# Feature-major chunks of a two-block kernel: from 256-column matmuls into one bank to 512-column and 256-column matmuls into two

## The chip, the cores and the metric

The kernel runs on one core of a Trainium2 chip. The metric is the device time of one execution in microseconds (us). One execution was profiled as well, and every row below is of that execution.

The engines are called as in the profile: PE is TensorE (matmuls), PEld its weight loads, DVE is VectorE, ACT is ScalarE, POOL is GpSimd, and SP issues the weight DMAs. Matmul results land in PSUM, which ACT and DVE read out.

## The reference

A sequence of 256 tokens with 1024 features goes through a first block and then twice through a hybrid layer. What matters here are projections of the normalised tokens:

```python
# first block
h = rms_norm(x, g_mix)
c_h, c_b, c_c, sq, sk, sv, xq, gate_pre = split(h @ w_in)
y_conv = (c_b * causal_depthwise_conv(c_c * c_h, conv_w)) @ w_conv_out
o_sb = stick_breaking_attention(heads(sq), heads(sk), heads(sv))   # 16 heads of 64
...
# hybrid layer, twice
fq, fk, fv, f_logit, rq, rk, rv, rg = split(x @ w_in)
fox_out = fox_attention(fq, fk, fv, log_sigmoid(f_logit + b_forget))  # 8 heads of 64
ret_out = silu(rg) * head_groupnorm(retention(rotary(rq), rotary(rk), rv))
x = layernorm(alpha * x + concat(fox_out, ret_out) @ w_out)
x = layernorm(alpha * x + square(relu(x @ w_ff1)) @ w_ff2)
```

## The kernel before

**Split operands.** Every float32 operand of a large matmul is held as two parts, hi (rounded by a cast to fp32r) and lo (the rest). A product is three matmuls: hi x hi, hi x lo and lo x hi. The activations of a stage lie in one tile `xT` of 128 partitions x 8 k-tiles x 2 parts x 256 tokens; `x[0]` is its hi part, `x[1]` its lo part, and `x[2]` both parts side by side, 512 elements for each k-tile.

**Weights.** `Stream` brings the weights in the order of use, in chunks of 1 MB and as two halves ("pieces"). For each piece ACT casts the raw data to `whi` (L218) and DVE subtracts to get `wlo` (L224). `tick()` is called between pieces of PE's work. It advances the side generators by one step (attention heads and the like) and then splits one or two more weight pieces. No scheduler moves anything: each engine runs its instructions in the order in which the code is written, and semaphores are the only waits.

**Feature-major chunks.** 32 chunks of 256 output features are computed with the features on the partitions by `stream_a` (L386): `sq`, `sk`, `ch`, `cc`, `cb` in each of four groups of the first block (loop `for i in range(4)`), and `fq`, `fk`, `rg`, two of each, in both hybrid layers. A chunk consists of two column tiles of 128 features (`nt` = 0 and 1). `unit_a` writes one column tile in 24 matmuls of 256 columns: for each of 8 k-tiles whi with `x[0]`, whi with `x[1]`, wlo with `x[0]`. Both column tiles go into the two halves of one PSUM bank, and the caller reads the bank directly (ACT casts, DVE subtracts or multiplies).

**PSUM.** `acc()` hands out four banks in turn. The pool takes the bank that has been free longest in program order, and PE waits until the bank's last reader is done. The chunks, the transposes `to_T` and the value products of the heads (`o = acc()` in `sb_pair` and `fox_pair`) all draw on these four. Scores and the heads' transposes use the other four banks (`aux`).

**One stick-breaking pair** (`sb_pair`, two heads). A step of PE writes the scores of both heads (12 matmuls, L348). ACT then computes abs, exp and ln (L611 to L613), DVE the sum `e`, a scan and a difference (`e`, `r`, `r`), ACT an exp (L619), DVE the causal mask (`r<-r,dmask`). Some ticks later PE transposes `r` (L628), ACT copies it to `pt`, and PE multiplies with the values (`acc<-pt,v`). In each group, the first pair's scores lie in the middle of `cc`, and its transposes in the middle of the next group's `sq`. There the second pair's scores follow right behind. The first pair's value product comes between the next `sk` and the next `ch`. The tick at the middle of a chunk calls the side steps ahead of the chunk's own eviction, so that what a pair computes on DVE stands in DVE's queue ahead of the chunk's readers.

**Wide chunks elsewhere.** The MLPs' up-projections use `stream_w` (L368): 16 matmuls of 512 columns, both banks first, and then 16 of 256.

Of the kernel before, what the change touches and what calls it, by code (L numbers as in the profile page):

```python
# [9 lines left out]
F32 = mybir.dt.float32  # L10
F32R = mybir.dt.float32r
BF16 = mybir.dt.bfloat16
AF = mybir.ActivationFunctionType
ALU = mybir.AluOpType
# [3 lines left out]
S = 256  # L18
# [235 lines left out]
def block_kernel(ctx: ExitStack, tc: tile.TileContext, a: dict, out: bass.AP, upto=None, dbg=None):  # L254
    nc = tc.nc
    ctx.enter_context(tc.manual_schedule())

    def pool(stack, name, bufs=1, side="left", space=None):
        kw = {} if space is None else {"space": space}
        return stack.enter_context(tc.tile_pool(name=name, bufs=bufs, side=side, reuse_waits="tile", **kw))  # L260
# [16 lines left out]
    def acc():  # L277
        return accp.tile([128, 512], F32, tag="acc", name="acc")
# [9 lines left out]
    def bank():  # L288
        assert cur_ps[0][1] == 1
        return cur_ps[0][0].tile([128, 512], F32, tag="bank", name="bank")  # L290
# [3 lines left out]
    W = Stream(nc, rp, wp, a["wpack"])  # L294
    sides = []

    def tick(n=1):
        for g in list(sides):
            if next(g, "end") == "end":
                sides.remove(g)  # L300
        W.pump(n)
# [17 lines left out]
    def act_set(name):  # L319
        if cur_set[0] != name:  # L320
            nc.scalar.preload_act_table_set(name)
            cur_set[0] = name

    def tt(o, x, y, op):
        nc.vector.tensor_tensor(o, x, y, op=op)  # L325

    def stt(o, x, s, y, op0, op1):
        nc.vector.scalar_tensor_tensor(out=o, in0=x, scalar=s, in1=y, op0=op0, op1=op1)  # L328

    def split(hi, lo, src):  # L330
        nc.scalar.copy(hi, src)  # L331
        tt(lo, src, hi.bitcast(F32), ALU.subtract)

    def split_scaled(hi, lo, src, s):
        nc.scalar.mul(hi, src, s)
        stt(lo, src, s, hi.bitcast(F32), ALU.mult, ALU.subtract)

    def mm3(o, lh, ll, rh, rl, first, last):
        nc.tensor.matmul(o, lhsT=lh, rhs=rh, start=first, stop=False, skip_group_check=True)  # L339
        nc.tensor.matmul(o, lhsT=lh, rhs=rl, start=False, stop=False, skip_group_check=True)  # L340
        nc.tensor.matmul(o, lhsT=ll, rhs=rh, start=False, stop=last, skip_group_check=True)  # L341
# [9 lines left out]
    def mm(o, l, r, first=True, last=True):  # L351
        nc.tensor.matmul(o, lhsT=l, rhs=r, start=first, stop=last, skip_group_check=True)  # L352

    def unit_a(o, w, nt, x):
        for k in range(8):
            ns = slice(nt * 128, nt * 128 + 128)
            mm3(o, w[0][:, k, ns], w[1][:, k, ns], x[0][:, k, :], x[1][:, k, :], k == 0, k == 7)
# [25 lines left out]
                W.free()  # L383
            evict(nt, ps[nt].rearrange("p (s t) -> p t s", s=2))

    def stream_a(key, x):  # L386
        w = W.get(key)
        p = acc()
        pv = p.rearrange("p (n t) -> p n t", n=2)
        unit_a(pv[:, 0, :], w, 0, x)  # L390
        tick()
        unit_a(pv[:, 1, :], w, 1, x)
        W.free()
        return pv

    def stream_b(key, x, evict=None):

        p = [acc(), acc()]
        for j in range(2):
            w = W.get((*key, j))  # L400
            for t in range(2):
                unit_b(p[t], w, t, x, 4 * j, j == 0, j == 1)
                if t:
                    W.free()
                if j and evict is not None:
                    evict(t, p[t])
                if not (j and t):
                    tick()
        return p
# [57 lines left out]
    def new_xT():  # L467

        xT = ap.tile([128, 8, 2, S], F32R, tag="xT", name="xT")
        return xT[:, :, 0, :], xT[:, :, 1, :], xT  # L470


    hT = new_xT()
# [13 lines left out]
    def turned(t, h, p):  # L487
        transposes(p, ht[t][:, hs[h]], 4)
        return p.rearrange("p (k t) -> p k t", k=4)
# [25 lines left out]
    p = turned(0, 0, acc())  # L515
# [7 lines left out]
    w = W.peek()  # L523
    term(p0, w, 0, 0, 0, 0, True)
    p = turned(0, 1, acc())
# [13 lines left out]
    w = W.peek()  # L539
# [6 lines left out]
    p = turned(1, 0, acc())  # L546
# [11 lines left out]
    p = turned(1, 1, acc())  # L558
# [26 lines left out]
    sp = pool(st1, "sb", side="right")  # L585
# [55 lines left out]
        split(osb[0][:, pair, :], osb[1][:, pair, :], o[:, 0:256])  # L641

    for i in range(4):
        p = stream_a(("sq", i), hT)
        split_scaled(qs[0], qs[1], p, 0.125)
        tick()
        p = stream_a(("sk", i), hT)
        split(kb[0], kb[1], p)
        tick()
        sides.append(sb_pair(i, 0, 2, 3))  # L650
        sides.append(sb_pair(i, 1, 6, 4))
        p = stream_a(("ch", i), hT)
        chs = sp.tile([128, 2, S], F32, tag="chs", name="chs")
        nc.scalar.copy(chs, p)
        tick()
        p = stream_a(("cc", i), hT)
        tt(u[:, :, 2:], p, chs, ALU.mult)
        cv = sp.tile([128, 2, S], F32, tag="cv", name="cv")
        for nt in range(2):
            ct = 2 * i + nt  # L660
            nc.vector.tensor_scalar(cv[:, nt, :], u[:, nt, 0:S], cw[:, ct, 0:1], None, op0=ALU.mult)
            stt(cv[:, nt, :], u[:, nt, 1:S + 1], cw[:, ct, 1:2], cv[:, nt, :], ALU.mult, ALU.add)
            stt(cv[:, nt, :], u[:, nt, 2:S + 2], cw[:, ct, 2:3], cv[:, nt, :], ALU.mult, ALU.add)
        tick()
        p = stream_a(("cb", i), hT)
        tt(cv, p, cv, ALU.mult)
        split(yc[0][:, 2 * i:2 * i + 2, :], yc[1][:, 2 * i:2 * i + 2, :], cv)
        tick()
# [45 lines left out]
    for n in range(2):  # L714
        ns = slice(512 * n, 512 * n + 512)
# [3 lines left out]
        def evict(t, p):  # L719
            tt(sg[:, t, :], p, sg[:, t, :], ALU.mult)  # L720
            tt(merged[:, t, ns], merged[:, t, ns], sg[:, t, :], ALU.add)
# [90 lines left out]
    for h in range(2):  # L812
        box = {}
        p = stream_b(("xk", h), memT)
# [3 lines left out]
        p = stream_b(("xq", h), hT)  # L818
        box["qn"] = qk_prep(p, gq, "q")
        tick()  # L820
        p = stream_b(("xv", h), memT)
# [255 lines left out]
    xT = x2T[0]  # L1077
    for l in range(2):
        st = ExitStack()
        p2 = pool(st, f"mix{l}")  # L1080

        def T(shape, dt, tag, bufs=1):
            return p2.tile(shape, dt, tag=tag, name=tag, bufs=bufs)
# [23 lines left out]
        for t in range(2):  # L1107
            pk = bank()
            for i in range(2):
                p = bank()  # L1110
# [68 lines left out]
        fp = pool(fst, f"fox{l}", side="right")  # L1179
# [54 lines left out]
            split(mix[0][:, pair, :], mix[1][:, pair, :], o[:, 0:256])  # L1234

        for i in range(2):
            p = stream_a((l, "fq", i), xT)
            split_scaled(fqs[0], fqs[1], p, 0.125)
            tick()
            p = stream_a((l, "fk", i), xT)  # L1240
            split(fkb[0], fkb[1], p)
            tick()
            for nt in range(2):
                fox.append(fox_pair(i, nt, *((0, 1, 4, 9), (0, 4, 7, 10), (1, 3, 6, 8), (4, 6, 8, 10))[2 * i + nt]))
            sides.extend(fox[-2:])
# [70 lines left out]
        rgt = T([128, 4, S], F32, "rkT")  # L1316
        ret = ret_side()
        sides.append(ret)
        for i in range(2):
            p = stream_a((l, "rg", i), xT)  # L1320
            s = rgt[:, 2 * i:2 * i + 2, :]
            act_set(SILU)
            nc.scalar.activation(s, p, AF.Silu)
            rgs[f"s{i}"] = s
            tick()
        nT = [None]
# [71 lines left out]
        xT = nT2[0]  # L1398
# [33 lines left out]
```

## Time and profile before

| | before |
|---|---|
| time, median of 3 runs | 1201.65 us (1201.48 to 1204.26) |
| the profiled execution | 1200.3 us, of which the span of the instructions is 1198.5 us |
| PE busy | 1189.2 us (99% of the span) |
| PEld busy | 1028.2 us (86%) |
| DVE busy | 790.7 us (66%) |
| ACT busy | 630.6 us (53%) |
| HBM | 181 GB/s over the span |
| granted PE clock | 0.999 of full speed |

"Busy" is a union of the instructions' intervals. A PE interval includes the way through the array and overlaps the next one, so the distance between starts tells PE's pace. A group's mean duration does not.

### The profile page before, as it was taken

What the parts mean: (1) busy time and instruction counts of PE and PEld (TensorE: products, weight loads), DVE (VectorE), ACT (ScalarE), POOL (GpSimd) and SP (SyncE); (2) the same over time, 40 slices, a digit from 0 to 9 for tenths busy, and PEclk for the clock granted to TensorE, in tenths of its full rate; (3) what the DMA queues carried; (4) which work ended last, traced back from release to release, by engine and by line L of the source; (5) the groups of instructions that cost most, each with busy time, mean ns of one, the idle gap of its engine ahead of it and who ended that gap; (6) DMA issues with size and microseconds to landing.
All of it is one profiled execution on the core that took longest, in us unless ns stands there. A gap on an engine that the chain in (4) does not pass through costs nothing.

```text
span 1198.5 us, 17236 instructions
## 1 busy us (share of the span) xinstructions
PE 1189.2 (99%) x6832; PEld 1028.2 (86%) x6832; DVE 790.7 (66%) x1036; ACT 630.6 (53%) x883; POOL 27.6 (2%) x46
## 2 busy tenths in 40 slices
PE   9999999999999999999999999999999999999997
PEld 6999988888888888888898888888889888888886
DVE  6678775656666667566566686656667668675563
ACT  6565556445554556455255555645535555664550
POOL 1000000000000100000000100000000010000000
PEclk9999999999999999999999999999999999999999
DMA  7654447654456566546454465655545436656530
GB/s 297 231 176 140 131 153 235 229 213 142 152 164 221 187 206 225 193 176 234 154 161 139 132 213 201 212 210 176 208 145 186 145 119 217 213 199 223 166 133 35
DMA packets 60354, 218.40 MB, mean 182 GB/s; under 512 B 6849, under 2 KB 7121, under 8 KB 60274
## 3 DMA queue, kind: packets, MB, share of 16 engines
q1 hardware_dynamic: 58176, 210.46, 51.6%
q0 software_dynamic: 1808, 6.45, 1.7%
q8 instruction: 53, 0.87, 0.3%
q10 hardware_dynamic: 290, 0.40, 0.1%
q14 instruction: 27, 0.22, 0.1%
HBM read 216.23 MB, written 1.05 MB: 181 GB/s over the span
## 4 chain that ended last, share of the span: by engine, by line
PE 99%; DVE 0%; POOLq 0%; issue 0%; DVEq 0%
PE acc L352 22%; PE acc L339 12%; PE acc L341 12%; PE acc L340 12%; PE bank L339 11%; PE bank L341 11%; PE bank L340 11%; PE acc L450 2%; PE bank L352 1%; PE aux L348 1%; PE aux L1222 0%; PE acc L435 0%; PE aux L628 0%; PE aux L340 0%; PE aux L341 0%; PE aux L339 0%
## 5 line engine op out<-in xcount | busy, mean ns | idle before, releaser
L224 DVE TENSOR_TENSOR wlo<-raw,whi 128x1024 fp32r<-128x1024 f32 x392 | 464.5, 1220 | 75.6 <-ACT whi L218 73.5
L218 ACT CAST whi<-raw 128x1024 fp32r<-128x1024 f32 x392 | 394.1, 1049 | 75.1 <-PE bank L341 36.9
L352 PE MATMUL acc<-xT,whi 128*128 128x512 f32 x672 | 160.2, 390 | 0.0
L339 PE MATMUL bank<-whi,hid 128*128 128x512 f32 (+1 forms) x388 | 150.6, 388 | 0.5 <-DVE x L328 0.5
L340 PE MATMUL bank<-wlo,hid 128*128 128x512 f32 (+1 forms) x388 | 150.3, 387 | 0.0
L341 PE MATMUL bank<-whi,hid 128*128 128x512 f32 (+1 forms) x388 | 150.1, 387 | 0.0
L339 PE MATMUL acc<-xT,whi 128*128 128x256 f32 x512 | 147.6, 288 | 0.0
L352 PEld LDWEIGHTS acc<-xT,whi 128*128 128x128 f32 x672 | 124.4, 188 | 24.8
L340 PE MATMUL acc<-xT,whi 128*128 128x256 f32 x512 | 144.8, 283 | 0.0
L341 PE MATMUL acc<-xT,wlo 128*128 128x256 f32 x512 | 144.7, 283 | 0.0
L922 ACT ACTIVATE r<-r 128x512 f32<-128x512 f32 x42 | 26.6, 633 | 157.5 <-DVE r L968 157.5
L339 PEld LDWEIGHTS acc<-xT,whi 128*128 128x128 f32 x512 | 98.0, 191 | 1.9 <-issue 1.0
L340 PEld LDWEIGHTS acc<-xT,whi 128*128 128x128 f32 x512 | 98.1, 192 | 0.2
L341 PEld LDWEIGHTS acc<-xT,wlo 128*128 128x128 f32 x512 | 98.0, 191 | 0.0
L352 PEld LDWEIGHTS acc<-xT,wlo 128*128 128x128 f32 x672 | 85.9, 191 | 3.0
L352 PE MATMUL acc<-xT,wlo 128*128 128x256 f32 x672 | 87.4, 283 | 0.0
L339 PEld LDWEIGHTS bank<-whi,hid 128*128 128x128 f32 x388 | 72.9, 188 | 15.0 <-DVE x L328 0.7
L341 PEld LDWEIGHTS bank<-whi,hid 128*128 128x128 f32 x388 | 72.8, 188 | 15.0
L968 DVE TENSOR_REDUCE r<-acc 128x256 f32<-128x512 f32 x84 | 55.5, 686 | 44.7 <-PE acc L352 44.7
L340 PEld LDWEIGHTS bank<-wlo,hid 128*128 128x128 f32 x388 | 72.9, 188 | 14.1
L325 DVE TENSOR_TENSOR hid<-r,hid 128x512 fp32r<-128x512 f32 x42 | 29.1, 692 | 84.8 <-ACT hid L331 84.8
L339 PE MATMUL acc<-whi,xT 128*128 128x512 f32 x208 | 83.4, 401 | 0.0
(293 smaller groups left out, 1734.3 us busy)
## 6 DMA issues: line engine op xcount, KB each, us to landing
raw<-in_wpack_dram SPq DMA_DIRECT2D x388, 512.0 KB, 4.5
raw<-in_wpack_dram SPq DMA_DIRECT2D x4, 528.0 KB, 4.6
gb<-in_ln_g_dram POOLq DMA_DIRECT2D x4, 512.0 KB, 3.8
bb<-in_ln_b_dram POOLq DMA_DIRECT2D x4, 512.0 KB, 5.8
x<-in_x_dram SPq DMA_DIRECT2D x3, 512.0 KB, 5.8
mem<-in_mem_dram SPq DMA_DIRECT2D x2, 512.0 KB, 6.1
cst<-in_c_dram POOLq DMA_DIRECT2D x1, 898.0 KB, 7.6
out_dram<-x SPq DMA_DIRECT2D x3, 256.0 KB, 2.1
```

Of the source, the lines that this page charges most:

```text
L218: nc.scalar.copy(hi, raw)
L224: self.nc.vector.tensor_tensor(lo, raw, hi.bitcast(F32), op=ALU.subtract)
L325: nc.vector.tensor_tensor(o, x, y, op=op)
L339: nc.tensor.matmul(o, lhsT=lh, rhs=rh, start=first, stop=False, skip_group_check=True)
L340: nc.tensor.matmul(o, lhsT=lh, rhs=rl, start=False, stop=False, skip_group_check=True)
L341: nc.tensor.matmul(o, lhsT=ll, rhs=rh, start=False, stop=last, skip_group_check=True)
L348: nc.tensor.matmul(o[:, h, :], lhsT=q[a][hs[h]], rhs=k[b][hs[h]], start=i == 0, stop=i == 2, skip_group_check=True)
L352: nc.tensor.matmul(o, lhsT=l, rhs=r, start=first, stop=last, skip_group_check=True)
L450: nc.tensor.transpose(o[:, k * 128:(k + 1) * 128], src[:, k * 128:(k + 1) * 128], ident)
L922: nc.scalar.activation(dst, src, AF.Relu)
L968: lambda nt, h: nc.vector.tensor_reduce(rv[:, nt, :], h, AX.X, ALU.add))
```

## The change

`stream_s` takes the place of `stream_a`. Each column tile gets a bank of its own, in which the two halves are the two products with the hi and the lo part of x. Eight matmuls of 512 columns (whi with `x[2]`) fill the bank, and eight of 256 columns (wlo with `x[0]`) accumulate onto the first half. After each column tile ACT copies the first half to an SBUF tile, and DVE adds the second half onto it. The middle `tick()` comes after the first column tile's eviction. The callers then read the SBUF tile in place of PSUM, and Silu runs in place on it.

```diff
--- before.py
+++ after.py
@@ -383,15 +383,26 @@
                 W.free()
             evict(nt, ps[nt].rearrange("p (s t) -> p t s", s=2))
 
-    def stream_a(key, x):
+    def stream_s(key, x, dst):
+
+        def evict(nt, h):
+            nc.scalar.copy(dst[:, nt, :], h[:, :, 0])
+            tt(dst[:, nt, :], h[:, :, 1], dst[:, nt, :], ALU.add)
+
         w = W.get(key)
-        p = acc()
-        pv = p.rearrange("p (n t) -> p n t", n=2)
-        unit_a(pv[:, 0, :], w, 0, x)
-        tick()
-        unit_a(pv[:, 1, :], w, 1, x)
-        W.free()
-        return pv
+        for nt in range(2):
+            p = acc()
+            ns = slice(nt * 128, nt * 128 + 128)
+            for k in range(8):
+                mm(p.rearrange("p (s t) -> p s t", s=2), w[0][:, k, ns], x[2][:, k], k == 0, False)
+            for k in range(8):
+                mm(p[:, 0:S], w[1][:, k, ns], x[0][:, k, :], False, k == 7)
+            if nt:
+                W.free()
+            evict(nt, p.rearrange("p (s t) -> p t s", s=2))
+            if not nt:
+                tick()
+        return dst
 
     def stream_b(key, x, evict=None):
 
@@ -641,19 +652,17 @@
         split(osb[0][:, pair, :], osb[1][:, pair, :], o[:, 0:256])
 
     for i in range(4):
-        p = stream_a(("sq", i), hT)
+        p = stream_s(("sq", i), hT, sp.tile([128, 2, S], F32, tag="st", name="st", bufs=2))
         split_scaled(qs[0], qs[1], p, 0.125)
         tick()
-        p = stream_a(("sk", i), hT)
+        p = stream_s(("sk", i), hT, sp.tile([128, 2, S], F32, tag="st", name="st", bufs=2))
         split(kb[0], kb[1], p)
         tick()
         sides.append(sb_pair(i, 0, 2, 3))
         sides.append(sb_pair(i, 1, 6, 4))
-        p = stream_a(("ch", i), hT)
-        chs = sp.tile([128, 2, S], F32, tag="chs", name="chs")
-        nc.scalar.copy(chs, p)
+        chs = stream_s(("ch", i), hT, sp.tile([128, 2, S], F32, tag="chs", name="chs"))
         tick()
-        p = stream_a(("cc", i), hT)
+        p = stream_s(("cc", i), hT, sp.tile([128, 2, S], F32, tag="st", name="st", bufs=2))
         tt(u[:, :, 2:], p, chs, ALU.mult)
         cv = sp.tile([128, 2, S], F32, tag="cv", name="cv")
         for nt in range(2):
@@ -662,7 +671,7 @@
             stt(cv[:, nt, :], u[:, nt, 1:S + 1], cw[:, ct, 1:2], cv[:, nt, :], ALU.mult, ALU.add)
             stt(cv[:, nt, :], u[:, nt, 2:S + 2], cw[:, ct, 2:3], cv[:, nt, :], ALU.mult, ALU.add)
         tick()
-        p = stream_a(("cb", i), hT)
+        p = stream_s(("cb", i), hT, sp.tile([128, 2, S], F32, tag="st", name="st", bufs=2))
         tt(cv, p, cv, ALU.mult)
         split(yc[0][:, 2 * i:2 * i + 2, :], yc[1][:, 2 * i:2 * i + 2, :], cv)
         tick()
@@ -1234,10 +1243,10 @@
             split(mix[0][:, pair, :], mix[1][:, pair, :], o[:, 0:256])
 
         for i in range(2):
-            p = stream_a((l, "fq", i), xT)
+            p = stream_s((l, "fq", i), xT, fp.tile([128, 2, S], F32, tag="st", name="st", bufs=2))
             split_scaled(fqs[0], fqs[1], p, 0.125)
             tick()
-            p = stream_a((l, "fk", i), xT)
+            p = stream_s((l, "fk", i), xT, fp.tile([128, 2, S], F32, tag="st", name="st", bufs=2))
             split(fkb[0], fkb[1], p)
             tick()
             for nt in range(2):
@@ -1317,10 +1326,9 @@
         ret = ret_side()
         sides.append(ret)
         for i in range(2):
-            p = stream_a((l, "rg", i), xT)
-            s = rgt[:, 2 * i:2 * i + 2, :]
+            s = stream_s((l, "rg", i), xT, rgt[:, 2 * i:2 * i + 2, :])
             act_set(SILU)
-            nc.scalar.activation(s, p, AF.Silu)
+            nc.scalar.activation(s, s, AF.Silu)
             rgs[f"s{i}"] = s
             tick()
         nT = [None]
```

**First place: DVE in the middle of the second group's `sq` chunk.** Before, this is DVE's order from the last weight piece ahead of the second pair's work (`e`, `r`) to the next `kb` (numbers are buffers, `acc` a PSUM bank, `aux` the scores):

```order
L224 TENSOR_TENSOR wlo_689<-raw_541,whi_688 128x1024
L328 SCALAR_TENSOR_TENSOR e_772<-aux_759,e_772 128x768
L615 SCALAR_TENSOR_TENSOR r_773<-smask_369,e_772 128x768
L325 TENSOR_TENSOR r_773<-aux_759,r_773 128x768
L224 TENSOR_TENSOR wlo_781<-raw_571,whi_780 128x1024
L328 SCALAR_TENSOR_TENSOR q1_374<-acc_725,q0_373 128x512
L325 TENSOR_TENSOR r_773<-r_773,dmask_370 128x2x256
L224 TENSOR_TENSOR wlo_781<-raw_623,whi_780 128x1024
L224 TENSOR_TENSOR wlo_844<-raw_661,whi_843 128x1024
L325 TENSOR_TENSOR kb1_376<-acc_818,kb0_375 128x512
```

In the changed kernel, from the same weight piece on; `st<-acc,st` is the new addition, `acc_674` and `acc_729` are the banks of the first and the second column tile of `sq`, and `acc_757` is that of the first of `sk`:

```order
L224 TENSOR_TENSOR wlo_642<-raw_516,whi_641 128x1024
L325 TENSOR_TENSOR st_673<-acc_674,st_673 128x256
L328 SCALAR_TENSOR_TENSOR e_715<-aux_702,e_715 128x768
L626 SCALAR_TENSOR_TENSOR r_716<-smask_369,e_715 128x768
L325 TENSOR_TENSOR r_716<-aux_702,r_716 128x768
L224 TENSOR_TENSOR wlo_724<-raw_539,whi_723 128x1024
L325 TENSOR_TENSOR st_673<-acc_729,st_673 128x256
L328 SCALAR_TENSOR_TENSOR q1_374<-st_673,q0_373 128x512
L325 TENSOR_TENSOR r_716<-r_716,dmask_370 128x2x256
L224 TENSOR_TENSOR wlo_724<-raw_586,whi_723 128x1024
L325 TENSOR_TENSOR st_756<-acc_757,st_756 128x256
L224 TENSOR_TENSOR wlo_777<-raw_619,whi_776 128x1024
```

The reader of `sq`'s one bank (`q1<-acc`) stood behind the pair's `e`, `r`, `r` and a weight piece; now the last reader of the second column tile's bank stands there. How many banks PE takes between this chunk and the next `ch` has changed too.

**PE at the same place.** Before, from the last matmul of `sk` (bank `acc_818`) over the values (`acc_875`) to the first of `ch` (`acc_886`), with the semaphores that each waits for:

```order
L341 MATMUL acc_818<-xT_124,wlo_538 128x256
L352 MATMUL acc_875<-pt_757,v_237 64x256 [waits Activation_49]
L352 MATMUL acc_875<-pt_757,v_237 64x128
L352 MATMUL acc_875<-pt_757,v_237 64x256
L352 MATMUL acc_875<-pt_757,v_237 64x128
L339 MATMUL acc_886<-xT_124,whi_619 128x256 [waits DVE_49]
```

In the changed kernel, from the end of the second column tile of `sq` (`acc_729`) to the first matmul of `ch` (`acc_815`):

```order
L352 MATMUL acc_729<-xT_124,wlo_462 128x256 x8
L352 MATMUL acc_757<-xT_124,whi_512 128x512 [waits DVE_49]
L352 MATMUL acc_757<-xT_124,whi_512 128x512 x7
L352 MATMUL acc_757<-xT_124,wlo_513 128x256 x8
L352 MATMUL acc_782<-xT_124,whi_512 128x512 [waits DVE_49]
L352 MATMUL acc_782<-xT_124,whi_512 128x512 x7
L352 MATMUL acc_782<-xT_124,wlo_513 128x256 x8
L352 MATMUL acc_803<-pt_700,v_237 64x256 [waits DVE_49,Activation_49]
L352 MATMUL acc_803<-pt_700,v_237 64x128
L352 MATMUL acc_803<-pt_700,v_237 64x256
L352 MATMUL acc_803<-pt_700,v_237 64x128
L352 MATMUL acc_815<-xT_124,whi_582 128x512 [waits DVE_49]
```

Between `sq` and `ch`, PE took the banks of `sq`, `sk` and the values, and `ch` the fourth. Now `acc_729`, two banks of `sk` and one of the values are four, and `acc_815` of `ch` is the fifth, which takes the bank of `acc_729`.

**Second place: PE at the second `rg` chunk of layer 0.** Before, from the middle of the chunk (bank `acc_6321`) over a value product of the fox heads (`acc_6346`) and the transposes of the normalised retention output for the first 128 tokens (`on_6261`), back to the chunk:

```order
L341 MATMUL acc_6321<-xT_5199,wlo_6012 128x256
L352 MATMUL acc_6346<-fpt_6224,ta_5919 64x256 [waits DVE_49]
L352 MATMUL acc_6346<-fpt_6224,ta_5919 64x128
L352 MATMUL acc_6346<-fpt_6224,ta_5919 64x256
L352 MATMUL acc_6346<-fpt_6224,ta_5919 64x128
L450 MATMUL acc_6353<-ident_62,on_6261 128x128 [waits Activation_49]
L450 MATMUL acc_6353<-ident_62,on_6261 128x128 x3
L339 MATMUL acc_6321<-xT_5199,whi_6011 128x256
```

In the changed kernel, from the last matmuls of the first column tile (`acc_6062`) on:

```order
L352 MATMUL acc_6062<-xT_4991,wlo_5764 128x256 x8
L352 MATMUL acc_6081<-fpt_5970,ta_5671 64x256 [waits DVE_49]
L352 MATMUL acc_6081<-fpt_5970,ta_5671 64x128
L352 MATMUL acc_6081<-fpt_5970,ta_5671 64x256
L352 MATMUL acc_6081<-fpt_5970,ta_5671 64x128
L461 MATMUL acc_6088<-ident_62,on_6007 128x128 [waits DVE_49]
L461 MATMUL acc_6088<-ident_62,on_6007 128x128 x3
L352 MATMUL acc_6100<-xT_4991,whi_5763 128x512 [waits DVE_49]
```

The rest of the chunk continued in a bank that it held already; its second column tile now starts a new bank (`acc_6100`) and waits for DVE. The transposes (`acc_6088`) waited for ACT and now wait for DVE.

## Rows read from the trace of the kernel before

**Rows 1.** The page: busy time by engine, and the chain that ended last

```profile
PE 1189.2 (99%) x6832; PEld 1028.2 (86%) x6832; DVE 790.7 (66%) x1036; ACT 630.6 (53%) x883; POOL 27.6 (2%) x46
...
PE 99%; DVE 0%; POOLq 0%; issue 0%; DVEq 0%
```

**Rows 2.** Timeline, TensorE: start, length, line, instruction, shape, count

```profile
521.44 3.79 PE L352 MATMUL acc<-xT,whi 128*128 128x512 f32 x16
525.06 2.08 PE L352 MATMUL acc<-xT,wlo 128*128 128x256 f32 x16
526.98 3.36 PE L352 MATMUL acc<-xT,whi 128*128 128x512 f32 x14
```

**Rows 3.** Windows, one group: PE, PEld, DVE, ACT, POOL, clock, DMA

```profile
52.80:86.00 33.20, 33.20 (x287) 32.28 (x286) 25.88 (x31) 19.98 (x25) 0.00 (x0) 1.00 0.43 140
```

**Rows 4.** Timeline, ScalarE and VectorE: a cast and a subtraction out of PSUM

```profile
79.75 0.37 ACT L331 CAST osbh<-acc 128x256 fp32r<-128x256 f32 x1
...
81.72 0.41 DVE L325 TENSOR_TENSOR osbl<-acc,osbh 128x256 fp32r<-128x256 f32 x1
```

**Rows 5.** Timeline, TensorE, from the first pair's transposes to the values

```profile
65.28 0.84 PE L628 MATMUL aux<-ident,r 128*128 128x128 f32 x6
66.05 0.91 PE L348 MATMUL aux<-kb,q 64*128 64x256 f32 x12
...
75.71 0.88 PE L352 MATMUL acc<-pt,v 128*64 128x256 f32 x8
```

**Rows 6.** Timeline, VectorE, the same stretch

```profile
64.50 0.68 DVE L325 TENSOR_TENSOR r<-r,dmask 128x512 f32<-128x512 f32 x1
...
67.38 0.68 DVE L325 TENSOR_TENSOR cv<-acc,cv 128x512 f32<-128x512 f32 x1
...
72.86 0.96 DVE L328 SCALAR_TENSOR_TENSOR e<-aux,e 128x768 f32<-128x768 f32 x1 [1.94 <-ACT e L613]
...
75.64 0.96 DVE L325 TENSOR_TENSOR r<-aux,r 128x768 f32<-128x768 f32 x1
76.52 1.22 DVE L224 TENSOR_TENSOR wlo<-raw,whi 128x1024 fp32r<-128x1024 f32 x1
77.65 0.68 DVE L328 SCALAR_TENSOR_TENSOR q<-acc,q 128x512 fp32r<-128x512 f32 x1
78.25 0.68 DVE L325 TENSOR_TENSOR r<-r,dmask 128x512 f32<-128x512 f32 x1
```

**Rows 7.** Timeline, ScalarE, the same stretch

```profile
68.09 0.62 ACT L331 CAST ych<-cv 128x512 fp32r<-128x512 f32 x1 [5.20 <-DVE cv L325]
...
70.26 0.82 ACT L611 ACTIVATE e<-aux 128x768 f32<-128x768 f32 x1
...
72.73 1.03 ACT L218 CAST whi<-raw 128x1024 fp32r<-128x1024 f32 x1
73.67 0.59 ACT L335 ACTIVATE q<-acc 128x512 fp32r<-128x512 f32 x1
76.64 0.85 ACT L619 ACTIVATE r<-r 128x768 f32<-128x768 f32 x1 [2.38 <-DVE r L325]
```

**Rows 8.** Timeline, VectorE and TensorE, around the rg chunks of layer 0

```profile
683.48 1.36 DVE L1294 TENSOR_SCALAR on<-acc,gmv,grs 128x128 f32<-128x128 f32 x4 [1.13 <-POOL grs L446]
...
677.60 0.36 PE L339 MATMUL acc<-xT,whi 128*128 128x256 f32 x1
...
683.52 0.88 PE L352 MATMUL acc<-fpt,ta 128*64 128x256 f32 x8
684.33 0.66 PE L450 MATMUL acc<-ident,on 128*128 128x128 f32 x4
```

**Rows 9.** TensorE at the start (timeline) and after its last matmul (windows)

```profile
1.19 3.59 PE L435 MATMUL acc<-wz 128*128 128x512 bf16 x8 [1.19 <-DVE wz L427]
...
1190.00:1194.00 4.00, 1.04 (x9) 1.00 0.00 0
1194.00:1198.50 4.50, 0.00 (x0) 0.72 0.32 117
```

## The prediction

> **What bounds the kernel now.** I read the page's busy times first, then its chain. PE is busy for 99% of the span, and the chain that ended last is PE alone [rows 1]: whatever PE saves is saved, and whatever PE newly waits is lost, microsecond for microsecond. So two questions are left: how fast PE runs either form of a chunk, and whether DVE and ACT empty PSUM banks early enough for the new form.
>
> The first is answered by the timeline of the MLP's chunks, which have exactly the matmuls that the change brings. Sixteen 512-column matmuls take 525.06 - 521.44 = 3.62 us from start to start, 0.226 each, and sixteen of 256 columns 526.98 - 525.06 = 1.92 us, 0.120 each [rows 2]. For the second I read what DVE does while one group runs: 25.88 us of 33.20, ACT 19.98 [rows 3]. There is room on average, but DVE comes in bursts, and in the burst of a stick-breaking pair it is level with PE: the mask `r<-r,dmask` ends at 64.50 + 0.68 = 65.18 [rows 6], and PE's transposes of that `r` start at 65.28 [rows 5]. There is 0.1 us of slack.
>
> **The change part by part.**
>
> *The matmuls.* Of 256 columns, a chunk had 48: 48 x 0.120 = 5.76 us. Now it has 16 x 0.226 + 16 x 0.120 = 5.54 us, or 2.77 us a column tile. That saves 0.21 us a chunk and, over 32 chunks (20 in the first block, 6 in each hybrid layer), **-6.7 us**. The rows are of the same shapes on the same engine at a granted clock of 1.00 [rows 3], so this is the surest term.
>
> Here a page speaks differently. The Trainium skill ("TensorE: Matmul & The Clock Gate", "Back-to-back issue gap") puts the distance of matmuls at the columns over 2.4 GHz and a fixed 2.5 ns or so. That gives about 0.109 and 0.216 us and an estimated saving of 0.04 us a chunk, 1.3 us in all; the sum below would end some 5 us later. The rows show 120 and 226 ns, about 13 ns beside the columns, so by them halving the number of matmuls is worth more than the page allows; I go by the rows.
>
> *The new evictions.* A chunk adds two copies on ACT and two additions on DVE. The trace has neither; the nearest rows are a cast and a subtraction out of PSUM of the same 128x256, 0.37 and 0.41 us [rows 4]. In a full queue instructions overlap somewhat (an `r` starts 0.60 us after a `q` of 0.68 [rows 6]), so I take 0.33 us for an addition that has something queued behind it. A group's five chunks add ten: 25.88 + 3.3 to 4.1 leaves DVE below 33.2 [rows 3]. By volume the additions are covered by DVE's idle time; the price lies where they stand in a burst.
>
> *First place, the first pair's mask.* From its scores to its transposes PE runs four column tiles, so it gets there 2 x 0.21 = 0.42 us sooner. DVE's path to the mask gets an addition (the first tile of `cc`, or the second, ahead of `u`) and a dependent step: about 0.45 us more. The slack was 0.1 [rows 5, 6]: 0.42 + 0.45 - 0.1 = 0.8 us of wait. I count it for the first group: **+0.8**. In the later groups PE has just waited elsewhere (below), which lets DVE catch up.
>
> *Second place, `sq`'s second bank.* This is the heart of the matter. PE reaches the next `ch` with the scores (0.91 us), the second tile of `sq` (2.77), all of `sk` (5.54) and the values (0.88) [rows 5]: 10.1 us, or 10.0 since each one's end overlaps the next start, after the second pair's scores start. Its bank is the fifth from the second tile of `sq`, so it must wait for that tile's addition. In DVE's queue the addition stands behind the pair's `e`, scan, `r` and a weight piece, exactly where `q<-acc` stood. That was at 77.65, which is 11.6 us after the scores' start at 66.05 [rows 5, 6]; with the addition's own 0.41 us, 12.0. The old chunk could afford it, since `ch` did not need this bank yet. So even if nothing else were late, PE waits 12.0 - 10.0 = **2.0 us**.
>
> I expect more. The pair's ACT work did not start with its scores: `e<-aux` began at 70.26 and stood behind `ych<-cv` at 68.09, which waited for DVE's `cv` at 67.38, behind the mask and two weight pieces [rows 6, 7]. That chain now gets two additions (`cb`'s tiles, 0.66 us), and ACT gets a copy of `sq`'s first tile ahead of `e` (0.3 us). Against it the mask ends 0.3 us sooner, since the chain ran a few tenths ahead until then. `e` moves from 72.86 to about 73.5, and the addition ends at about 77.65 + 0.41 + 0.7 = 78.8. PE's scores start at about 65.8 and it arrives at 75.8: a wait of **3.0 us**, in each of three groups (the last group has no next `sq`, and the first `ch` no pair ahead of it). **+9.0**.
>
> *Right behind it, the second tile of `ch`.* It takes the bank of `sk`'s first tile. ACT's `q` (0.59) needs the late addition, the exp (0.85) stands behind it on ACT, then a weight cast (1.0) [rows 7], DVE's half of that piece (1.13 to the next start [rows 6]), and only then the addition for `sk`'s first tile (0.41): 4.0 us from the moment that PE starts `ch`. PE is through the first tile in 2.8. **+1.1** each, three times: **+3.3**. It is nothing if DVE does not keep this order, but no one reorders the queue.
>
> *Third place, `rg`.* The second `on`, normalised out of a PSUM bank, ends at 683.48 + 1.36 = 684.84. PE went from the chunk's middle at 677.60 over 48 matmuls to the values at 683.52 and the transposes at 684.33 [rows 8]. Now it needs 5.54 + 0.81 = 6.35 us and gets to the transposes at 683.95, and these take the bank that the second `on` has to leave: 0.7 to 0.9 us. The second tile of the second `rg` then takes the bank of the first chunk's second tile, whose addition stands behind that `on` and a weight piece: 684.84 + 1.13 + 0.41 = 686.4 against PE's 684.84 and 0.4 us of transposes, 1.1. Together 1.8 to 2.0 a layer, **+3.7** in two.
>
> *Costed at nothing.* The other chunks (`cc`, `cb`, fox `q` and `k`) take banks whose readers have nothing of a pair's burst ahead of them; their cover is the column tile of 2.77 us that PE runs meanwhile. If that were short by as much as at `ch`'s second tile in all eight fox chunks, it would be 9 us more. The callers' reads from SBUF replace reads from PSUM of the same size; 0 to 0.2 us each, in DVE's idle time.
>
> *Sum.* -6.7 + 0.8 + 9.0 + 3.3 + 3.7 = +10.1 us. The profiled execution took 1200.3 us (span 1198.5), so 1210.4; it lies 1.35 below the median of the runs, and I predict **1212 us**.
>
> **The rivals.**
>
> *Clean gain (1195).* Only the matmuls count, and the banks come free in time: 1201.65 - 6.7. For it: DVE is busy for only 66% [rows 1]. It decides if the addition of `sq`'s second tile stands ahead of the scan in time, that is if it ends more than 2.0 us sooner than the rows put it; I see nothing that moves it. Chance 0.07.
>
> *Waits that about pay for the gain (1200 to 1204).* The second place costs its lower bound, 3 x 2.0, ACT's delay being absorbed, and the others little (up to 3.7): 1201.65 - 6.7 + 6.0 + (0 to 3.7). For it: PE's wait lets DVE catch up, so the waits may not add. Against it: the second tile of `ch` follows from the first wait. Chance 0.10.
>
> *The clock falls too (1217).* After the last matmul, PE's granted clock went from 1.00 to 0.72 on average over the next stretch, and at the start eight matmuls of 512 columns took 3.59 us, 0.45 each and twice the later pace, so at the lower of the two levels, 1.2 GHz [rows 9]. If each of the three waits of 3 us brought such a stretch, each would lose half of it, 1.8 us: +5.4. Against it: at the end PE had nothing left at all, and here it pauses in the midst of dense work. Chance 0.11. The Trainium skill (same page, "HAM oscillation — how this bites in real kernels") says that idle time between bursts of matmuls can send the clock back; no row of before has such a gap to test it.
>
> *Forecast*, slower by waits at a full clock: 0.72.
>
> **How the numbers follow.** About 0.3% (3.6 us) can be told from no change. The first rival is faster, the second nearly all the same; a twentieth of the others is shared among these: faster 0.08, same 0.10, slower 0.82. The forecast's own range is 1206 to 1216: three waits at 2.0 instead of 3.0 take 3 us off, the rest at half another 3.5, and a shortfall at some fox chunks adds 4. For 8 in 10 I leave the clean gain and half of the second rival outside and take in the clock's lower half: 1203.5 to 1217.5.
>
> **What would show it.** Right: PE busy falls to about 1182.5 us while the span grows; PE's rows show three waits of about 3 us ahead of `ch`'s first matmul, ended by DVE's addition into `st`, each followed by one of about 1 us; two waits near each `rg`; 512-column matmuls at 0.226 us. Wrong: a PE busy that does not fall (the pace), waits at `ch` of 2 us or less (ACT's delay), none at all (order of the banks), or granted clocks below 0.9 in those groups. A wait at many other chunks would mean that the additions are slower out of PSUM than the row of 0.41.

## The result and the profile after

| | before | after |
|---|---|---|
| time, median of 4 runs | 1202.95 us (1201.48 to 1204.27) | 1214.51 us (1214.21 to 1216.68) |
| ratio | | 1.0105, 95% interval 1.0089 to 1.0120 |
| span of the profiled execution | 1198.5 us | 1212.3 us |

The change makes the kernel slower by 1%. The time lies inside the stated range (1203.5 to 1217.5) and 2.5 us above the 1212 predicted. Executions of every version differ by some 3.5 us in their first 12 us (last section), so spans of experiments are compared below from the first `sq` chunk on: 1165.9 us before (1198.5 - 32.6), 1179.7 after (1212.3 - 32.6), +13.8. By their times, two of the four executions before and one of the four after had the longer start; among the others the change costs 12.8 us (1214.2 to 1214.6 against 1201.5 and 1201.7). One execution of all, of the version with the old form for `sq`, `sk` and `rg`, took 3057.6 us and is left out of its ratio.

The page of the changed kernel, to be held against [rows 1]:

```profile
PE 1190.6 (98%) x6320; PEld 1005.0 (83%) x6320; DVE 815.2 (67%) x1100; ACT 648.8 (54%) x943; POOL 27.6 (2%) x46
...
PE 91%; DVE 5%; ACT 2%; issue 1%; POOL 0%; POOLq 0%; DVEq 0%
```

PE's busy time has not fallen but risen by 1.4 us, and the chain that ended last is no longer PE alone: DVE has 5% of it and ACT 2%. PE's waits (engine, line, what it waited for, total, times, longest), without the two that both kernels have (1.2 us for `wz` at the start, and 0.5 us in the last MLP, at 1189.35 us before). The kernel before has no others:

```profile
PE acc L352 <- DVE st L325: 8.8, 3, 3.0
PE acc L352 <- DVE rkT L325: 1.6, 2, 0.8
PE acc L461 <- DVE on L1303: 1.4, 2, 0.7
PE aux L639 <- DVE r L325: 0.6, 1, 0.6
```

These four new kinds of wait amount to 12.4 us. They stand at the three places that the prediction named: three at `ch`, two pairs at `rg`, one at the first pair's transposes.

PE's timeline at the first two places (what stood there before is [rows 5]):

```profile
65.11 0.87 PE L639 MATMUL aux<-ident,r 128*128 128x128 f32 x6 [0.59 <-DVE r L325]
...
75.34 0.88 PE L352 MATMUL acc<-pt,v 128*64 128x256 f32 x8
79.06 3.03 PE L352 MATMUL acc<-xT,whi 128*128 128x512 f32 x8 [2.84 <-DVE st L325]
81.89 1.80 PE L352 MATMUL acc<-xT,wlo 128*128 128x256 f32 x8
83.53 1.98 PE L352 MATMUL acc<-xT,whi 128*128 128x512 f32 x8
...
86.29 0.82 PE L639 MATMUL aux<-ident,r 128*128 128x128 f32 x6
```

The transposes of the first pair wait 0.59 us for DVE's mask. PE ends the values at about 76.2 and starts `ch` at 79.06, after 2.84 us of waiting for an addition into `st`. Then comes what the forecast left to a rival: the eight 512-column matmuls take 81.89 - 79.06 = 2.83 us, where 1.81 is usual (8 x 0.226), and the eight of 256 columns 1.64 where 0.96 is usual. The granted clock says why (window, its length, busy time and count of PE, clock, DMA share, GB/s):

```profile
75.30:79.00 3.70, 0.92 (x9) 1.00 0.00 0
79.00:80.00 1.00, 0.94 (x4) 1.00 0.26 57
80.00:83.00 3.00, 3.00 (x12) 0.50 0.41 156
83.00:84.00 1.00, 1.00 (x7) 0.79 0.41 94
84.00:88.00 4.00, 4.00 (x26) 1.00 0.68 237
```

At 80.0 us, 0.9 us after the gap's end, the clock goes from 1.00 to 0.50, 1.2 in place of 2.4 GHz. It comes back about when the chunk's second tile starts: the 0.79 of the fourth row is 0.50 up to 83.4 us and 1.00 behind it. From the start of `ch` to that of the transposes behind it PE takes 86.29 - 79.06 = 7.23 us. DVE in the same stretch, against [rows 6]:

```profile
64.37 0.69 DVE L325 TENSOR_TENSOR r<-r,dmask 128x512 f32<-128x512 f32 x1
...
73.79 0.96 DVE L328 SCALAR_TENSOR_TENSOR e<-aux,e 128x768 f32<-128x768 f32 x1 [1.88 <-ACT e L624]
...
76.58 0.96 DVE L325 TENSOR_TENSOR r<-aux,r 128x768 f32<-128x768 f32 x1
77.45 1.22 DVE L224 TENSOR_TENSOR wlo<-raw,whi 128x1024 fp32r<-128x1024 f32 x1
78.59 0.42 DVE L325 TENSOR_TENSOR st<-acc,st 128x256 f32<-128x256 f32 x1
...
82.51 0.42 DVE L325 TENSOR_TENSOR st<-acc,st 128x256 f32<-128x256 f32 x1
```

The mask, `e`, `r` and the weight piece have their old order. `e` begins 0.93 us later than before (72.86), the addition that `ch` waits for stands behind them all at 78.59, and that of `sk`'s first tile comes at 82.51. The latter ends at 82.93, and PE wanted its bank only at 83.53. At full clock PE would have been there at 79.06 + 2.77 = 81.83: the slow clock has hidden a wait of 1.1 us.

PE at `rg` of layer 0, against [rows 8], and then in the middle of the output projection:

```profile
693.90 0.88 PE L352 MATMUL acc<-fpt,ta 128*64 128x256 f32 x8
695.45 0.66 PE L461 MATMUL acc<-ident,on 128*128 128x128 f32 x4 [0.67 <-DVE on L1303]
696.91 2.12 PE L352 MATMUL acc<-xT,whi 128*128 128x512 f32 x8 [0.81 <-DVE rkT L325]
...
707.40 0.39 PE L340 MATMUL bank<-wlo,mixh 128*128 128x512 f32 x1
707.79 0.50 PE L341 MATMUL bank<-whi,mixl 128*128 128x512 f32 x1
708.13 0.40 PE L339 MATMUL bank<-whi,mixh 128*128 128x512 f32 x1
```

Two waits of 0.67 and 0.81 us at the two predicted steps, and 0.3 us in all at two matmuls of the projection, which come 0.39 and 0.34 us after their forerunners in place of 0.23. The first of the two reads `mixl`, which DVE writes from 707.05 to 707.74 us.

### The profile page after: what moved, and what is told of

Read it like the earlier page. It is cut to its first block, busy times and chain, and to the rows that moved or that the text cites. A ratio compares the mean times of both kernels' runs of the same rounds, so it can differ in the third digit from the quotient of the medians.

```text
span 1212.3 us, 16319 instructions
## 1 busy us (share of the span) xinstructions
PE 1190.6 (98%) x6320; PEld 1005.0 (83%) x6320; DVE 815.2 (67%) x1100; ACT 648.8 (54%) x943; POOL 27.6 (2%) x46
## 3 DMA queue, kind: packets, MB, share of 16 engines
HBM read 216.23 MB, written 1.05 MB: 179 GB/s over the span
## 4 chain that ended last, share of the span: by engine, by line
PE 91%; DVE 5%; ACT 2%; issue 1%; POOL 0%; POOLq 0%; DVEq 0%
PE acc L352 31%; PE bank L339 11%; PE bank L341 11%; PE bank L340 11%; PE acc L339 6%; PE acc L341 6%; PE acc L340 6%; PE acc L461 2%; PE bank L352 1%; DVE wlo L224 1%; PE aux L348 1%; DVE r L626 1%; PE aux L1231 0%; DVE e L328 0%; PE acc L446 0%
## 5 line engine op out<-in xcount | busy, mean ns | idle before, releaser
L352 PE MATMUL acc<-xT,whi 128*128 128x512 f32 x1184 | 294.9, 397 | 10.4 <-DVE st L325 8.8
L352 PEld LDWEIGHTS acc<-xT,whi 128*128 128x128 f32 x1184 | 218.5, 190 | 55.1 <-DVE st L325 9.5
L352 PEld LDWEIGHTS acc<-xT,wlo 128*128 128x128 f32 x1184 | 157.3, 192 | 8.5
L352 PE MATMUL acc<-xT,wlo 128*128 128x256 f32 x1184 | 159.8, 284 | 0.0
L339 PE MATMUL acc<-whi,xT 128*128 128x512 f32 x208 | 83.4, 401 | 0.0
L341 PE MATMUL acc<-whi,xT 128*128 128x512 f32 x208 | 81.2, 390 | 0.0
L340 PE MATMUL acc<-wlo,xT 128*128 128x512 f32 x208 | 81.1, 390 | 0.0
L341 PEld LDWEIGHTS acc<-whi,xT 128*128 128x128 f32 x208 | 39.0, 188 | 8.5
L339 PEld LDWEIGHTS acc<-whi,xT 128*128 128x128 f32 x208 | 39.1, 188 | 8.2 <-issue 0.5
L340 PEld LDWEIGHTS acc<-wlo,xT 128*128 128x128 f32 x208 | 39.1, 188 | 7.4
L339 PE MATMUL bank<-whi,xT 128*128 128x512 f32 (+2 forms) x120 | 40.4, 337 | 0.0
```

## The experiments

**Filling the gap with work.** In groups 1 to 3, PE gets matmuls that nobody reads, ahead of `ch`:

```diff
+        if i:
+            fill = aux()
+            for _ in range(13):
+                mm(fill[:, 0:512], hT[0][:, 0, 0:128], hT[2][:, 0])
         chs = stream_s(("ch", i), hT, ...)
```

> The changed kernel with 13 extra matmuls of 512 columns ahead of ch in groups 1 to 3, into a bank of the scores' pool that nobody reads; they are 13 x 0.226 = 2.9 us and lie in the time in which PE waits for the bank of sq's second tile (2.84 to 3.04 us in the changed kernel's trace). Theory (wait, and a clock fall behind it): the wait turns into work, the granted clock stays at 1.00 through ch, ch's two tiles take 5.7 us in place of 7.24, and the wait of about 1.1 us at ch's second tile, which the slow clock had covered, comes to light. Net 3 x (1.1 - 1.55) = -1.4 us: about 1213. Rival 1 (the second tile of ch never had a wait): -4.7, about 1210. Rival 2 (ch is slow for another reason, a port or DVE's writes, and the clock only looks so): ch stays at 7.2 us, no gain, or 0.3 us more.

PE's timeline and two of the windows:

```profile
76.27 3.24 PE L352 MATMUL aux<-xT 128*128 128x512 f32 x13
79.35 2.00 PE L352 MATMUL acc<-xT,whi 128*128 128x512 f32 x8
81.18 1.11 PE L352 MATMUL acc<-xT,wlo 128*128 128x256 f32 x8
83.12 2.12 PE L352 MATMUL acc<-xT,whi 128*128 128x512 f32 x8 [0.83 <-DVE st L325]
```

```profile
75.30:79.00 3.70, 3.70 (x22) 1.00 0.00 0
...
80.00:83.00 3.00, 2.29 (x14) 1.00 0.41 156
```

The span from the first `sq` is 1178.3 us (1211.1 - 32.8), 1.4 less than the changed kernel's; the ratio to before is 1.012 (1.0101 to 1.0140), not to be told from the changed kernel's. `ch`'s first eight matmuls take 1.83 us, the clock stays at 1.00, and the second tile now waits 0.83 us (2.6 us in three groups), as the theory had it: 1.1 less the 0.3 by which `ch` starts later. So the clock's fall hangs on the gap, not on `ch`'s matmuls or on DVE's writes beside them, and both rivals fall.

The mean granted clocks of all executions bear this out: 0.998 or 0.999 in the four with the filled gap, 0.995, 0.997, 0.995 and 0.999 in the four of the changed kernel. A fall as in the windows above loses 3.00 x 0.50 + 1.00 x 0.21 = 1.7 us of clock, 0.0014 of the span. So the changed kernel's fourth execution (1216.7 us, not profiled) had one fall at most: the clock fell behind all three gaps of the profiled execution, but not in every execution.

**ACT empties the banks.** In the first block ACT copies both halves and DVE adds them in SBUF (the hybrid layers keep the lines marked with a minus):

```diff
-            nc.scalar.copy(dst[:, nt, :], h[:, :, 0])
-            tt(dst[:, nt, :], h[:, :, 1], dst[:, nt, :], ALU.add)
+            e = tmp()
+            nc.scalar.copy(e, h.rearrange("p t s -> p s t"))
+            tt(dst[:, nt, :], e[:, 0, :], e[:, 1, :], ALU.add)
```

> The changed kernel, but in the first block ACT copies both halves out of PSUM in one instruction and DVE adds them in SBUF, so no bank waits for DVE's addition. Theory (what counts is the place in the in-order queues, not the engine that reads): the wait ahead of ch's first tile goes, since ACT's copy of sq's second tile stands ahead of the exp; but ACT's copy of sk's first tile stands behind q on ACT, which needs DVE's late addition, so ch's second tile now waits about 3 us in its place and the clock falls there: within 1.5 us of the changed kernel, about 1213 to 1215. Rival (the bank waits because DVE is too slow a reader; taken from DVE, it is free): the 13.7 us of the three places go, about 1201.

PE, and ACT around the copy that PE waits for:

```profile
76.03 2.11 PE L352 MATMUL acc<-xT,whi 128*128 128x512 f32 x8
...
82.00 2.75 PE L352 MATMUL acc<-xT,whi 128*128 128x512 f32 x8 [2.91 <-ACT ev L391]
84.56 1.91 PE L352 MATMUL acc<-xT,wlo 128*128 128x256 f32 x8
```

```profile
79.17 0.63 ACT L335 ACTIVATE q<-st 128x512 fp32r<-128x512 f32 x1 [3.85 <-DVE st L325]
79.71 0.83 ACT L635 ACTIVATE r<-r 128x768 f32<-128x768 f32 x1
80.44 1.03 ACT L218 CAST whi<-raw 128x1024 fp32r<-128x1024 f32 x1
81.38 0.58 ACT L391 COPY ev<-acc 128x512 f32<-128x512 f32 x1
```

The ratio is 1.0134 (1.0110 to 1.0158), the span from the first `sq` 1180.3 us (1212.8 - 32.5). `ch` starts at 76.03 without a wait, and its second tile waits 2.91 us for ACT's copy, which stands behind `q`, an exp and a weight cast. `q` needs DVE's late sum. Behind this wait the clock falls too: 0.54 from 83 to 86 us, and 2.56 us (82.00 to 84.56) for eight wide matmuls. One of its other three executions took 1222.2 us at a mean clock of 0.989, where the profiled one has 0.994, so the clock was low for longer there; where is not known. Which engine reads the bank made no difference here; the place of the reader in its in-order queue did.

**The old form where the banks were late.** `sq`, `sk` and `rg` go back to one bank and 256 columns; the other 20 chunks keep the new form:

```diff
-        p = stream_s(("sq", i), hT, sp.tile(...))
+        p = stream_a(("sq", i), hT)
-        p = stream_s(("sk", i), hT, sp.tile(...))
+        p = stream_a(("sk", i), hT)
...
-            s = stream_s((l, "rg", i), xT, rgt[:, 2 * i:2 * i + 2, :])
+            p = stream_a((l, "rg", i), xT)
+            s = rgt[:, 2 * i:2 * i + 2, :]
             act_set(SILU)
-            nc.scalar.activation(s, s, AF.Silu)
+            nc.scalar.activation(s, p, AF.Silu)
```

> Old form (one bank, 256-column matmuls) for sq, sk and rg, new form for the other 20 chunks. Theory (all the loss is waits at the banks of sq, sk and rg, with the clock fall behind them): those waits go; 20 chunks save 20 x 0.165 = 3.3 us, the first pair's mask still makes PE wait some 0.6 us in the first group, and the bank of kb may cost 0 to 0.3 us in three groups: about 1200.3 to 1201.2 against 1203, just faster than before. Rival (the new form loses by itself, by its evictions or its change of widths): slower than before, above 1204.

PE's waits, without that for `wz`:

```profile
PE bank L339 <- DVE x L328: 0.5, 1, 0.5
PE aux L649 <- DVE r L325: 0.5, 1, 0.5
```

The ratio is 0.9991 (0.9978 to 1.0003), but it mixes the two starts: by their times, six of these eleven executions had the longer one, and four of the 17 before. Start by start, all lie lower than before, by some 2 us: 1197.6 to 1199.1 against 1199.9 to 1201.2, and 1201.3 to 1201.8 against 1204.0 to 1204.6. In the traces the stretch from the first `sq` is 2.2 us shorter (1196.6 - 32.9 = 1163.7). The waits at `ch` and `rg` are gone and 0.5 us at the first pair's mask is left. The new form does not lose by itself.

**The old form for `rg` alone**, by the same edit:

> The changed kernel with the old form for rg alone (4 chunks). Theory (the waits at rg's banks and the late last addition cost 3.7 us in the two layers: 1.4 for the second on, 1.6 for the first rg's addition, 0.7 at the output projection that the late rg delays): these go, and 4 x 0.16 = 0.65 of gain goes with them; -3.0 us, a span of 1209.3 against 1212.3, all of it in the two layers behind the first block. Rival (they are covered elsewhere, so that only the gain is lost): +0.65 us.

Ratio 1.0065 (1.0046 to 1.0083). The span from the first `sq` is 1175.8 us (1208.3 - 32.5), 3.9 less than the changed kernel's, where 3.0 was expected, and all of it lies in the two layers. By the starts of PE's groups, layer 0 loses 0.74 us at the transposes, 1.05 at the second tile and 0.37 in the projection, the next layer 0.76, 1.06 and 0.37, 4.35 in all, from which the gain of four chunks goes off. The expectation added up the waits as PE's view lists them; from start to start a gap costs 0.1 to 0.2 us more, since the matmul ahead of it runs out without a successor (one of 256 columns lasts 0.28 us in the trace, and in a row the next starts 0.12 us behind it).

**The old form for `sk` alone**, so that PE takes one bank less between `sq` and `ch`:

> The changed kernel with the old form for sk alone, so that one bank less is taken between sq and ch. sq's second addition stays behind the burst in DVE's queue. Theory (the wait belongs to the count of banks and the place in the queue): ch's first tile takes the bank of sq's first tile and does not wait; ch's second tile takes that of sq's second, free at about the time that PE gets there (0 to 0.3 us of wait); the first tile of cc now takes sk's bank, whose last reader kb stands behind q, the mask and two weight pieces in DVE's queue and ends about 1.8 us too late, in three groups. If a wait of 1.8 us leaves the clock alone: -13.7 + 0.65 + 5.4 = -7.6, a span of 1204.7; if the clock falls behind it as behind the 3 us: up to 4.6 more, 1209.3. Rival (the wait belongs to sq's two-bank form itself): it stays at ch, span 1212 to 1213.

PE and DVE at `cc`, and two of the windows:

```profile
88.46 2.14 PE L352 MATMUL acc<-xT,whi 128*128 128x512 f32 x8 [1.56 <-DVE kb L325]
90.44 1.10 PE L352 MATMUL acc<-xT,wlo 128*128 128x256 f32 x8
```

```profile
87.72 0.69 DVE L325 TENSOR_TENSOR kb<-acc,kb 128x512 fp32r<-128x512 f32 x1
```

```profile
86.00:88.40 2.40, 0.90 (x9) 1.00 0.25 56
...
89.40:92.40 3.00, 3.00 (x27) 1.00 0.87 264
```

The span from the first `sq` is 1172.6 us (1209.1 - 36.5), 7.1 less than the changed kernel's (7.6 expected); the ratio is 1.0067 (1.0045 to 1.0089). Nothing waits at `ch` any more; the first tile of `cc` waits 1.56 us for `kb`, 4.8 in three groups. So the wait moves with the count of banks, as the theory says. Behind these waits the granted clock stayed at 1.00, and eight wide matmuls took 1.98 us. That is the profiled execution, with a mean clock of 0.998; three of the other four had 0.996 and one 0.999, so whether the clock stays up behind such waits every time is open.

**The new banks and evictions with narrow matmuls.** 24 matmuls of 256 columns a tile:

```diff
-                mm(p.rearrange("p (s t) -> p s t", s=2), w[0][:, k, ns], x[2][:, k], k == 0, False)
+                mm(p[:, 0:S], w[0][:, k, ns], x[0][:, k, :], k == 0, False)
+                mm(p[:, S:2 * S], w[0][:, k, ns], x[1][:, k, :], k == 0, k == 7)
```

> The changed kernel with its banks and evictions, but 24 matmuls of 256 columns a tile in place of 8 of 512 and 8 of 256. It measures the gain of the wide matmuls alone. Theory: waits stay, PE comes to them 0.25 us later, so each is 0.2 to 0.3 us shorter; the matmuls cost 32 x 0.165 = 5.3 us more (by the tile times of the traces; by the prediction's rows 6.7): about +4 to +5, 1218.5 to 1219.5. Rival (the gain of the wide form is that of the Trainium skill's pace, 1.3 us in all, and the rest of the traces' difference is something else): +0.5 us, about 1215.

Here the second half of a bank is started while the first is still being summed, so this version does not compute the reference's result and stands here for its time alone. Ratio 1.0152 (1.0132 to 1.0172); from the first `sq` the span is 1182.6 us (1218.7 - 36.1), 2.9 more than the changed kernel's. A `cc`-to-transposes stretch of two tiles takes 5.86 us against 5.69-5.70, so 0.16 us a chunk or 5.1 in 32. Against that stand waits that are 2.1 us shorter (7.4 for 8.8 at `ch`, 1.0 for 1.4 at the second `on`, 0.3 for 0.6 at the mask): 5.1 - 2.1 = 3.0. The expectation missed by more than 1 us because it took off too little for the waits; the pace is what it said. The clock fell behind these shorter waits of 2.59, 2.41 and 2.41 us as well; the window behind the first:

```profile
84.30:87.70 3.40, 3.40 (x18) 0.50 0.40 142
```

**The mask ahead of the convolution.** The version with the old form for `sq`, `sk` and `rg`, with one tick moved:

```diff
         p = stream_s(("cc", i), hT, sp.tile(...))
+        tick()
         tt(u[:, :, 2:], p, chs, ALU.mult)
...
-        tick()
         p = stream_s(("cb", i), hT, sp.tile(...))
```

> The version with the old form for sq, sk and rg and the new one for the other 20 chunks (its span was 1196.6 us against 1198.5 before), with the tick behind cc moved ahead of cc's convolution, so that DVE does the first pair's mask ahead of u and cv. Theory: the last new wait, 0.5 us at the first pair's transposes in the first group, goes: a span of 1196.1, 2.4 us below before, ratio about 0.998. Rival (cv is then late for cb's product, which moves the second pair's work and the bank of kb, where PE came only 0.2 us after the bank was free): waits of 0.3 to 1 us appear at cc in three groups, span 1197 to 1199.

PE's waits, without that for `wz`:

```profile
PE bank L339 <- DVE x L328: 0.5, 1, 0.5
PE acc L352 <- DVE q L328: 0.2, 1, 0.2
```

The ratio is 0.9973 (0.9960 to 0.9986): faster than before, if by little, and so among the executions of either start (1197.4 to 1198.7 against 1200.0 to 1201.5, and 1200.9 to 1201.6 against 1203.7 to 1205.0). From the first `sq` the span is 1163.2 us (1199.5 - 36.3), 2.7 less than before and 16.5 less than the changed kernel. The mask's wait is gone and only 0.2 us at one bank has come for it. The span itself was not the 1196.1 expected, because this execution's start took 3.4 us longer than that of the version it was reckoned from (36.3 against 32.9 us).

## Why the prediction was right, and where its sum was off

The profiled executions differ by 13.8 us, where the sum was 10.1. By the starts of PE's groups in both traces:

| term | predicted | measured |
|---|---|---|
| matmuls, 32 chunks | -6.7 | -5.1 |
| first pair's mask | +0.8 | +0.8 |
| `ch`'s first tile, three groups | +9.0 | +9.0 (2.91, 3.04, 3.04) |
| `ch`'s second tile, three groups | +3.3 | 0 |
| clock behind the gap, three groups | 0 | +4.7 |
| `rg` and what follows, two layers | +3.7 | +4.3 |
| sum | +10.1 | +13.7 |

**Right: the bound and the mechanism.** PE waits where the fifth bank comes due, for as long as the walk through DVE's queue gave. Both halves of the 3.0 us are seen: DVE's own burst, and the delay of ACT's `e`, predicted at 73.5 and measured at 73.79. The experiment with the old form for `sq`, `sk` and `rg` takes the waits away with the late banks, the one with `sk` alone moves them, and the one in which ACT empties the banks moves them as well.

**Mis-sized: the matmuls.** 0.21 us a chunk was worked out from sixteen matmuls of one width in a row. A column tile here changes width after every eight. Behind the values of a pair, the old form's 48 matmuls take 99.42 - 93.57 = 5.85 us and the new form's 32 take 102.97 - 97.28 = 5.69:

```profile
93.57 0.39 PE L339 MATMUL acc<-xT,whi 128*128 128x256 f32 x1
...
99.42 0.82 PE L628 MATMUL aux<-ident,r 128*128 128x128 f32 x6
```

```profile
97.28 2.11 PE L352 MATMUL acc<-xT,whi 128*128 128x512 f32 x8
...
102.97 0.82 PE L639 MATMUL aux<-ident,r 128*128 128x128 f32 x6
```

The difference is 0.16. Where a chunk follows a chunk (the first group's `sk`, 38.35 to 44.11 us before and 38.18 to 43.77 after), they are 5.76 and 5.59: the old form's 5.76 was right, and the new form's 5.54 was 0.05 too low. The experiment with narrow matmuls measured 0.16 as well. The pace of the Trainium skill ("TensorE: Matmul & The Clock Gate", "Back-to-back issue gap"), by which the estimate was 0.04 a chunk, is further off.

**The step that failed: a full clock behind the waits.** The rival with the falling clock had 0.11, and its mechanism came: after the gap of 2.84 us at 76 us the granted clock went to 0.50, and `ch` took 7.23 us; behind the other two gaps it took 7.25 and 7.26, where 5.70 is usual. The price was 1.55 us each, not 1.8. The Trainium skill ("TensorE: Matmul & The Clock Gate", "HAM oscillation — how this bites in real kernels") says that idle time between bursts of matmuls can send the clock back; this trace agrees, in all three groups. The forecast argued against it that PE pauses "in the midst of dense work"; the dense work ahead did not keep the clock. It did stay up behind gaps of 0.6 to 1.6 us in the profiled executions.

**What the two did to each other.** The wait at `ch`'s second tile was right as a mechanism (0.83 us appears as soon as the gap is filled) but costs nothing beside a slow clock, under which PE comes to the bank late anyway. The forecast's +3.3 and the measured +4.7 are thus two prices for the same stretch, and the rival was wrong to add them. That the total came within 2.5 us is in part luck: a wait that stood in the sum and did not show was replaced by a slow clock that the forecast had put at nothing, at nearly the same price.

**Too low: `rg`.** The two waits were there (0.74 and 1.05 from start to start); not foreseen was that the last addition makes the gated `rg` late for the output projection as well, 0.37 us a layer.

**PE's busy time**, forecast at 1182.5, was 1190.6. It was named as a sign of a wrong pace, but only 1.6 of these 8.1 us are the pace. Busy time counts matmuls at half clock in full (+4.7); the rest, some 1.8 us, is put down here to the matmul ahead of each gap, which runs out without a successor, and was not measured by itself.

## What to carry to other kernels

Before a stage gets more PSUM banks per step, count which earlier bank each later step takes over, and find its last reader's place in its engine's queue; an engine that is idle a third of the time can still be 3 us late there. A gap on PE is dearer than its length when the clock falls behind it, here by half again: in the profiled executions it fell behind every gap of 2.4 to 3.0 us and stayed up behind those of 0.2 to 1.6. The length of the gap alone does not settle it: one execution of the changed kernel had one fall at most (mean clock 0.999), and two of the version without such gaps (the old form for `sq`, `sk` and `rg`) had a mean clock of 0.996, where its profiled execution has 0.999. Where the clock fell in those two is not known. The wide form pays where the bank that comes due has an early reader: in 20 of the 32 chunks, with the mask moved ahead of the convolution, it made the kernel 0.3% faster, and in all 32 it made it 1% slower.

## What the runs showed of the hardware that was not expected

**The start has two lengths.** The four small matmuls behind the first eight take 2.0 us in some executions and 3.8 in others, in the kernel before as in every version. TensorE's timeline of the changed kernel, and then of the version with the mask moved:

```profile
1.19 3.59 PE L446 MATMUL acc<-wz 128*128 128x512 bf16 x8 [1.19 <-DVE wz L438]
4.75 2.03 PE L451 MATMUL aux<-grow,one 1*128 1x512 f32 x4
```

```profile
1.19 3.59 PE L456 MATMUL acc<-wz 128*128 128x512 bf16 x8 [1.19 <-DVE wz L448]
4.72 3.78 PE L461 MATMUL aux<-grow,one 1*128 1x512 f32 x4
```

The slower start goes on at half pace up to about 13 us, so the first `sq` chunk begins at 36.3 us in place of 32.6. The difference fits the two clusters in all the runs (1199.9 to 1201.7 and 1203.7 to 1205.0 for the kernel before), and every profiled execution lies on the side of its start. What decides between them was not tried.

**The granted clock has no entry for the start.** In both stretches the windows give a granted clock of 1.00, although eight 512-column matmuls take 3.59 us; behind the gaps at `ch` the same column shows 0.50. The trace's record of the granted clock begins only at 4.91 us in the changed kernel and at 13.09 us in the version with the mask moved, and a window without an entry prints 1.00. The pace changes at that place: with the mask moved, three 512-column matmuls from 8.43 us take 1.25 us, 0.42 each, and six from 13.79 us take 1.39, 0.23 each. The record begins at 12.6 to 13.9 us in the three profiled executions with the longer start, and at 4.7 to 5.5 us in the six others. So the longer start is a later rise of the clock, and the pace shows it where the granted clock does not.
